# A hybrid retention and DeltaNet layer on one core: query norms from transposes, clears on GpSimd, and a priority for the last attention head

## The chip, the cores and the metric

The kernel runs on one core of a Trainium2 chip. The metric is the device time of one execution in microseconds (us); the time of a kernel is the median of its runs.

Five engines work side by side, each through its own instructions in order: TensorE (PE in the profile: matrix products and transposes into PSUM), VectorE (DVE), ScalarE (ACT), GpSimd (POOL) and SyncE (SP), which here only issues transfers (DMA). Semaphores make one engine wait for another.

## The reference

One encoder layer, batch 1, 256 tokens, width 2048, all in 32-bit floats:

```python
h = rms_norm(x, norm_mix_g)
x = x + hybrid_mixer(h, ...)           # retention and gated DeltaNet
h = rms_norm(x, norm_x_g)
x = x + cross_attention(h, rms_norm(mem, norm_mem_g), w_q, w_kv, w_o)   # 4 heads of 512
h = rms_norm(x, norm_ffn_g)
x = x + jnp.square(jax.nn.relu(h @ w_ff1)) @ w_ff2                      # hidden 8192
out = rms_norm(x, norm_final_g)
```

The change touches the gated DeltaNet and the cross-attention. In the DeltaNet each of 16 heads of width 128 normalises its queries and keys, and then runs the delta rule in chunks of 64 tokens:

```python
gqkv = silu(causal_conv(gqkv, conv_w))
gq, gk, gv = jnp.split(gqkv, ...)
gq = gq * lax.rsqrt(jnp.sum(gq * gq, axis=-1, keepdims=True) + 1e-6) * 128 ** -0.5
gk = gk * lax.rsqrt(jnp.sum(gk * gk, axis=-1, keepdims=True) + 1e-6)
yg = gated_delta_chunked(gq, gk, gv, log_a, beta)   # a triangular solve in each chunk
```

So a sum of squares over the 128 features of a head is needed for each of 256 tokens, of the queries and of the keys. The cross-attention is softmax(q k^T / sqrt(512)) v over 256 memory tokens, head by head, followed by the product with w_o.

## The kernel before

**Weights.** Every dense weight (w_in, w_out, w_xq, w_xkv, w_xo, w_ff1, w_ff2) comes from memory in pieces of 1 MB by the function `fetch`: SP issues the transfer into `raw` (three buffers), ACT rounds each half of it to a high part `whi` (L117, 128x1024), and DVE makes the low part `wlo = raw - whi` (L118). Each of both has three buffers. TensorE multiplies high by high, high by low and low by high, so that products keep nearly the precision of 32 bits. In `blocks`, which makes 256 output features as two PSUM banks s0 and s1, one L200 (a weight's high part by high and low activations side by side, 512 columns) and one L201 (the weight's low part by the high activations, 256 columns) are done for each of 16 input blocks and each of the two banks. The halves of 1024 columns feed eight such pairs. `chunk` does the same with L158 to L160 where the tokens stand on the partitions.

**What sets the order.** The program is written stage by stage, and a scheduler lays out each engine's instructions beforehand by priority and by its own estimate of the time. An instruction's priority is its place in the program, and `tc.high_priority(offset=n)` moves it n places ahead: 100000 in `fetch`, so weights are split as early as their buffers allow, and 50000 for the evacuations of the PSUM banks. Everything else fills what is left. Small results go through `bank()`, one of four PSUM banks under the tag b; s0 and s1 have two each.

**The DeltaNet's stream.** `gdn_stream` handles a group of four heads as two pairs, and runs four times. For each pair it projects queries, keys and values of two heads by `blocks`, convolves them (`conv_silu`, with a 128x256 buffer under the tag acc), and holds keys and queries in `kq`, features on the partitions, and the values in `vt`. Then, for each head: `kh` and `kl`, the high and low parts of keys and queries; `sq`, the square of the queries by ACT (L679, under the tag acc as well); two products of `sq` with a column of `ones` (L686), which sum over the partitions into a few columns of a bank, `ssq`; the products of keys with keys and queries (L688, L690); and the keys' sums of squares from the diagonals (L694). After both heads, `qe4` is made of `ssq` by DVE, `nk` (the keys' lengths) by GpSimd (L704), and, for each head again, ACT copies pieces to `cmp_l` and to the sparse tiles `pair32` and `pair64` (L718 to L725), TensorE transposes `vt` into a bank (L729), and ACT scales it by `nk` into `r4` (L732). `qe4` is read in `gdn_core`, which runs while the next groups' projections stream.

**The triangular solve.** `gdn_blocks` writes `cmp_l` to memory (`scr_l`), reads it back in another layout (`lw`), sets `tw` to the unit matrix (L744, L745) and solves by 31 pairs of DVE instructions (L750, L752). `tw` is one buffer, cleared in each of the four groups. The sparse tiles `pair32`, `pair64`, `t64`, `u64` and `u128` are cleared once (L629), when the pool `mix` opens on memory that the stage before held; `ko` of that stage is still being written to `kt_d` then.

**The cross-attention.** For each of 4 heads: queries, scores, softmax, transposes of the weights `pt`, and then, for two halves d2 of the head's 512 features, twelve value products into one bank (by `three`, L129 to L131; high and low parts of values `vv` and of `pt`), a copy by ACT into the high part of the head's activations `q` (L1080), and a subtraction by DVE for the low part (L1081). Four heads' activations are the input of `blocks` on w_xo, in `residual_pass`; after the last head nothing else is left for TensorE but that product, which reads the first half's activations for its thirteenth and fourteenth blocks of input. `split` is the helper for such a copy and subtraction, and `square_sum` the one for a square with an accumulated sum by ACT.

Of the kernel before, what the change touches and what calls it, by code (L numbers as in the profile page):

```python
# [10 lines left out]
F32 = mybir.dt.float32  # L11
F32R = mybir.dt.float32r
I32 = mybir.dt.int32
AF = mybir.ActivationFunctionType
ALU = mybir.AluOpType
AX = mybir.AxisListType

P = 128
D = 2048
S = 256  # L20
NT = S // P
# [3 lines left out]
GH, GD = 16, 128  # L25
XH, XD = 4, 512
EPS = 1e-6
# [25 lines left out]
def trunk(ctx: ExitStack, tc: tile.TileContext, x_f, mem_f, positions, lead_f, small_f, w_in, ret_gn_g, w_out, w_xq,  # L53
# [3 lines left out]
    act, vec, pool, pe = nc.scalar, nc.vector, nc.gpsimd, nc.tensor  # L57
# [65 lines left out]
    def split(dst, src, at=slice(None)):  # L123
        h, l = (a[:, at] for a in dst)
        act.activation(h, src, AF.Copy)
        vec.tensor_sub(l, src, h.bitcast(F32))

    def three(o, lhs, rhs, first, last):
        pe.matmul(o, lhs[0], rhs[0], start=first, stop=False)  # L129
        pe.matmul(o, lhs[0], rhs[1], start=False, stop=False)  # L130
        pe.matmul(o, lhs[1], rhs[0], start=False, stop=last)  # L131
# [102 lines left out]
    ident = cp.tile([P, P], F32, name="ident")  # L234
    ones = cp.tile([P, P], F32, name="ones")
# [31 lines left out]
    def square_sum(acc, src):  # L267
        junk = sm.tile([P, 512], F32, name="junk", tag="junk", bufs=1)
        act.activation(junk[:, :src.shape[1]], src, AF.Square, accum_out=acc)
# [354 lines left out]
    mx = mixer.enter_context(tc.tile_pool(name="mix", bufs=2))  # L624


    def sparse(nm, *shape):
        t = mx.tile([P, 4, *shape], F32, name=nm, bufs=1)
        vec.memset(t, 0.0)  # L629
        return t  # L630

    pair32, pair64 = sparse("pair32", P), sparse("pair64", P)
# [15 lines left out]
    def gdn_stream(grp):  # L648

        heads = []  # L650
        qe4 = mx.tile([P, 4, NT], F32, name="qe4", tag="qe4", bufs=2)
        for pr in range(2):
            h0 = grp * 4 + pr * 2
            dec = mx.tile([P, 2, 384], F32, name="dec", tag="dec", bufs=1)
            nc.sync.dma_start(dec, dec_d[h0:h0 + 2].rearrange("h p n -> p h n"))
            kq = mx.tile([P, 2, 2, S], F32, name="kq", tag="kq", bufs=1)
            vts = []
            for part, c0, bofs in ((1, C_GQ, 0), (0, C_GK, 16), (2, C_GV, 32)):
                def evac(b, ps, part=part, bofs=bofs):
                    if part < 2:  # L660
                        conv_silu(bofs + h0 + b, ps, kq[:, b, part, :])
                    else:
                        vt = mx.tile([P, S], F32, name="vt", tag="vt", bufs=2)
                        conv_silu(bofs + h0 + b, ps, vt)
                        vts.append(vt)
                blocks(h1, w_in[0], c0 + h0 * GD, 2, evac)
            if pr == 0:
                finish_steps()
                cmp_l = mx.tile([P, 8, 32], F32, name="cmp_l", tag="cmp", bufs=1)
                r4 = mx.tile([P, 4, NT, GD], F32, name="r4", tag="r4", bufs=1)  # L670
            grams = []
            ssk = mx.tile([P, 2, NT], F32, name="ssk", tag="ssk", bufs=2)
            for b in range(2):
                kh = mx.tile([P, 2, S], F32R, name="kh", tag="kh", bufs=2)
                kl = mx.tile([P, 2, S], F32R, name="kl", tag="kl", bufs=2)
                sq = mx.tile([P, S], F32, name="sq", tag="acc", bufs=2)
                act.activation(kh, kq[:, b], AF.Copy)
                vec.tensor_sub(kl, kq[:, b], kh.bitcast(F32))
                act.activation(sq, kq[:, b, 1], AF.Square)  # L679
                g0, g1 = bank(), bank()  # L680
                g0v = g0.rearrange("p (a n) -> p a n", a=2)
                g1v = g1[:, 0:256].rearrange("p (a n) -> p a n", a=2)
                if b == 0:
                    ssq = g1[:, 256:260].rearrange("p (b i) -> p b i", b=2)
                for t in range(NT):
                    pe.matmul(ssq[:, b, t:t + 1], sq[:, t * P:(t + 1) * P], ones[:, :1], start=True, stop=True)  # L686
                for n, (l, r) in enumerate(((kh, kh), (kh, kl), (kl, kh))):
                    pe.matmul(g0v, l[:, 0, 0:P], r, start=n == 0, stop=n == 2)  # L688
                for n, (l, r) in enumerate(((kh, kh), (kh, kl), (kl, kh))):
                    pe.matmul(g1v, l[:, 0, P:S], r[:, :, P:S], start=n == 0, stop=n == 2)  # L690
                grams.append((g0v, g1v))
                for t, src in enumerate((g0v[:, 0, 0:P], g1v[:, 0, :])):
                    dj = sm.tile([P, S], F32, name="dj", tag="bo", bufs=2)[:, :P]
                    vec.scalar_tensor_tensor(dj, src, 1.0, ident, op0=ALU.mult, op1=ALU.mult,  # L694
                                             accum_out=ssk[:, b, t:t + 1])
            ske = mx.tile([P, 2, NT], F32, name="ske", tag="ske", bufs=2)
            vec.tensor_scalar(ske, ssk, EPS, None, op0=ALU.add)
            vec.tensor_scalar(qe4[:, 2 * pr:2 * pr + 2, :], ssq, EPS * GD, EPS * EPS * GD,
                              op0=ALU.mult, op1=ALU.add)
            sc = mx.tile([P, 2, NT], F32, name="sc", tag="sc", bufs=2)  # L700
            vec.reciprocal(sc, ske)
            vec.tensor_mul(sc, sc, beta[:, :, h0:h0 + 2].rearrange("p t h -> p h t"))
            nk = mx.tile([P, 2, NT], F32, name="nk", tag="nk", bufs=2)
            pool.tensor_tensor(nk.rearrange("p b t -> p (b t)"), ske.rearrange("p b t -> p (b t)"), half_pow[:, :4], op=ALU.pow)  # L704
            for b in range(2):
                h, slot = h0 + b, pr * 2 + b
                g0v, g1v = grams[b]

                alt = mx.tile([P, 2, 384], F32, name="alt", tag="alt", bufs=4)
                vec.scalar_tensor_tensor(alt[:, :, 0:S], g0v, sc[:, b, 0:1],  # L710
                                         dec[:, b, 0:256].unsqueeze(1).to_broadcast([P, 2, 256]),
                                         op0=ALU.mult, op1=ALU.mult)
                vec.scalar_tensor_tensor(alt[:, :, S:384], g1v, sc[:, b, 1:2],
                                         dec[:, b, 256:384].unsqueeze(1).to_broadcast([P, 2, P]),
                                         op0=ALU.mult, op1=ALU.mult)
                for q in range(4):
                    ps_ = slice(32 * q, 32 * q + 32)
                    act.activation(cmp_l[ps_, 2 * slot:2 * slot + 2, :], diag(alt)[ps_, :, 32 * q:32 * q + 32], AF.Copy)  # L718

                for t in range(NT):  # L720
                    for a in range(2):
                        to, at = 64 * t + 32 * a, 64 * a
                        act.activation(pair32[to:to + 32, slot, to:to + 32],
                                       diag(alt)[at:at + 32, t, at + 32:at + 64], AF.Copy)
                    act.activation(pair64[64 * t:64 * t + 64, slot, 64 * t:64 * t + 64], diag(alt)[0:64, t, 64:P], AF.Copy)  # L725

                vps = bank()
                for t in range(NT):
                    pe.transpose(vps[:, t * P:(t + 1) * P], vts[b][:, t * P:(t + 1) * P], ident)  # L729
                r = r4[:, slot, :, :]  # L730
                for t in range(NT):
                    act.activation(r[:, t, :], vps[:, t * P:(t + 1) * P], AF.Copy, scale=nk[:, b, t:t + 1])  # L732
                heads.append(alt)
        return heads, cmp_l, r4, qe4

    def gdn_blocks(heads, cmp_l):
# [4 lines left out]
        for q in range(4):  # L741
            nc.sync.dma_start(lw[8 * q:8 * q + 8], scr_l[32 * q:32 * q + 32, :].rearrange("m (g n) -> g m n", g=8))
        tw = mx.tile([32, 32, 32], F32, name="tw", tag="tw", bufs=1)
        vec.memset(tw, 0.0)  # L744
        vec.memset(tw.rearrange("p i c -> p (i c)")[:, ::33], 1.0)  # L745
        for j in range(31):
            n = 31 - j
            pr = mx.tile([32, 272], F32, name="pr", tag="pr", bufs=2)
# [287 lines left out]
    for h in range(XH):  # L1036
# [34 lines left out]
        quad = quad_a()  # L1071
        for d2 in range(2):
            ops = bank()
            ov = ops.rearrange("p (d s) -> p d s", d=2)
            for d in range(2):
                c0 = (2 * d2 + d) * P
                for m in range(NT):
                    three(ov[:, d, :], [a[:, m, c0:c0 + P] for a in vv], [a[:, m, :] for a in pt], m == 0, m == 1)
            qh, ql = (a[:, 2 * d2:2 * d2 + 2, :] for a in quad)
            act.activation(qh, ov, AF.Copy)  # L1080
            vec.tensor_sub(ql, ov, qh.bitcast(F32))  # L1081
        att.append(quad)

    h3, rstd3 = residual_pass(att, w_xo[0], G_FFN, "n3")
# [130 lines left out]
```

## Time and profile before

| what | before |
|---|---|
| median of 3 runs | 2069.61 us (2069.28 to 2069.83) |
| the profiled execution | 2069.25 us |
| its span, first to last instruction | 2067.5 us |
| mean granted TensorE clock | 0.999 |
| memory traffic | 194 GB/s over the span |

The stages by the trace, with the time that TensorE was busy in each:

| stretch, us | stage | TensorE busy, us |
|---|---|---|
| 0 to 110 | memory's norm, first values | 108.54 of 110 |
| 110 to 200 | values and keys of the memory | 90.00 of 90 |
| 200 to 1060 | mixer: retention, DeltaNet, gates | 858.97 of 860 |
| 1060 to 1370 | w_out, cross-attention, w_xo | 309.74 of 310 |
| 1370 to 2067 | MLP, last norm | 689.45 of 697 |

A row of the trace reads: start and duration in us, engine, line, operation, out<-in, the tile's shape, how many; and in brackets how long the engine stood idle before it and what it then waited for. In a view of groups the last column is the idle time before the group. The profile splits one 32-bit product of L686 into two passes. Where matmuls follow closely, each is shown with its whole duration, though the next begins before it ends.

### The profile page before, as it was taken

Reading aid. Unit: us, or ns where it says so; the run is one execution under the profiler, and the core shown is the slowest. Engines: PE = TensorE matmul, PEld = TensorE weight load, DVE = VectorE, ACT = ScalarE, POOL = GpSimd, SP = SyncE. Lnnn points to the kernel's source line nnn. Section 1 sums busy time; section 2 is a strip of 40 time slices with the busy share of each in tenths; the row PEclk is TensorE's granted clock in tenths of the full one; section 3 lists DMA queues with packets and bytes.
Section 4 is the critical chain, followed back from the end, with each engine's and each line's share of the span. In section 5 each row is a group of like instructions: output and inputs, shape, how many; then the busy total and the mean of one; then the engine's idle time right before and its main releaser. Section 6 shows DMA issues by size and latency. Waiting matters only on the chain.

```text
span 2067.5 us, 28359 instructions
## 1 busy us (share of the span) xinstructions
PE 2056.7 (99%) x10954; PEld 1773.0 (86%) x10954; DVE 1420.2 (69%) x2262; ACT 1096.9 (53%) x1739; POOL 30.7 (1%) x37
## 2 busy tenths in 40 slices
PE   9999999999999999999999999999999999999998
PEld 7888888988888888888888898888888888888887
DVE  5887778779667875878567666776556556655654
ACT  5665764675456555755455555554344434434444
POOL 0000000000000000000000000000000000000000
PEclk9999999999999999999999999999999999999999
DMA  9688656555555655565577654689566566566654
GB/s 325 204 261 279 191 179 214 154 187 190 178 171 184 196 178 168 186 188 171 166 223 239 188 184 142 201 202 232 201 187 194 189 194 193 187 200 186 198 187 142
DMA packets 329222, 405.22 MB, mean 196 GB/s; under 512 B 34928, under 2 KB 239360, under 8 KB 328960
## 3 DMA queue, kind: packets, MB, share of 16 engines
q1 hardware_dynamic: 328656, 402.74, 62.5%
q8 instruction: 85, 1.39, 0.3%
q10 hardware_dynamic: 432, 0.69, 0.1%
q14 instruction: 49, 0.40, 0.1%
HBM read 389.74 MB, written 11.55 MB: 194 GB/s over the span
## 4 chain that ended last, share of the span: by engine, by line
PE 99%; DVE 0%; issue 0%; ACT 0%; DMA 0%; POOLq 0%; POOL 0%; ACTq 0%
PE s L200 34%; PE s L201 18%; PE s L159 13%; PE s L158 13%; PE s L160 13%; PE s L384 1%; PE s L386 1%; PE s L385 1%; PE b L781 1%; PE b L688 1%; PE b L814 1%; PE b L130 0%; PE b L129 0%; PE b L131 0%; PE b L690 0%; PE b L686 0%
## 5 line engine op out<-in xcount | busy, mean ns | idle before, releaser
L118 DVE TENSOR_TENSOR wlo<-raw,whi 128x1024 fp32r<-128x1024 f32 x696 | 850.7, 1223 | 495.5 <-ACT whi L117 488.4
L117 ACT ACTIVATE whi<-raw 128x1024 fp32r<-128x1024 f32 x696 | 737.0, 1060 | 698.4 <-PE s L160 347.3
L200 PE MATMUL s<-q,whi 128*128 128x512 f32 x3072 | 1056.7, 391 | 0.3 <-DVE q L1081 0.3
L201 PE MATMUL s<-q,wlo 128*128 128x256 f32 x3072 | 837.5, 281 | 1.0 <-DVE wlo L118 1.0
L200 PEld LDWEIGHTS s<-q,whi 128*128 128x128 f32 x3072 | 566.9, 188 | 109.5 <-DVE q L1081 0.5
L201 PEld LDWEIGHTS s<-q,wlo 128*128 128x128 f32 x3072 | 576.4, 188 | 14.9 <-DVE wlo L118 1.7
L159 PE MATMUL s<-wlo,q 128*128 128x512 f32 (+1 forms) x1200 | 470.4, 392 | 0.0
L160 PE MATMUL s<-whi,q 128*128 128x512 f32 (+1 forms) x1200 | 467.4, 390 | 0.0
L158 PE MATMUL s<-whi,q 128*128 128x512 f32 (+1 forms) x1200 | 427.5, 390 | 0.0
L158 PEld LDWEIGHTS s<-whi,q 128*128 128x128 f32 x1200 | 225.0, 188 | 47.2
L160 PEld LDWEIGHTS s<-whi,q 128*128 128x128 f32 x1200 | 225.4, 188 | 45.7
L159 PEld LDWEIGHTS s<-wlo,q 128*128 128x128 f32 x1200 | 225.5, 188 | 45.3
L207 ACT ACTIVATE bo<-s 128x256 f32<-128x256 f32 x192 | 72.9, 379 | 123.2 <-PE s L201 110.1
L208 DVE TENSOR_TENSOR bo<-bo,s 128x256 f32<-128x256 f32 x192 | 79.9, 416 | 42.0 <-ACT bo L207 41.7
L641 DVE SCALAR_TENSOR_TENSOR acc<-bo,small,acc 128x255 f32<-128x255 f32 (+1 forms) x144 | 66.8, 480 | 3.1 <-ACT acc L638 1.2
L750 DVE TENSOR_TENSOR pr<-lw,tw 32x31 f32<-32x31 f32 (+15 forms) x124 | 40.4, 326 | 8.3 <-DMA lw<-scr_l 6.2
L752 DVE TENSOR_TENSOR tw<-tw,pr 32x31 f32<-32x31 f32 (+15 forms) x124 | 40.5, 327 | 2.0
L1128 DVE SCALAR_TENSOR_TENSOR res<-s,rstd3q,res 128x512 f32<-128x512 f32 (+1 forms) x32 | 22.3, 736 | 12.0 <-PE s L160 12.0
L915 ACT ACTIVATE gth<-s 128x512 f32<-128x512 f32 x32 | 19.0, 593 | 18.1 <-PE s L160 15.1
L1115 DVE SCALAR_TENSOR_TENSOR hs<-bo 128x256 f32<-128x256 f32 x64 | 27.0, 423 | 1.1
L1118 DVE TENSOR_TENSOR q<-hs,q 128x256 fp32r<-128x256 f32 x64 | 26.7, 418 | 0.0
L1117 ACT ACTIVATE q<-hs 128x256 fp32r<-128x256 f32 x64 | 26.1, 409 | 0.6 <-DVE hs L1115 0.6
(310 smaller groups left out, 1178.1 us busy)
## 6 DMA issues: line engine op xcount, KB each, us to landing
raw<-w_in SPq DMA_DIRECT2D x143, 1024.0 KB
raw<-w_ff SPq DMA_DIRECT2D x128, 1024.0 KB
raw<-w_xkv SPq DMA_DIRECT2D x29, 1024.0 KB
raw<-w_out SPq DMA_DIRECT2D x16, 1024.0 KB
raw<-w_xq SPq DMA_DIRECT2D x16, 1024.0 KB
raw<-w_xo SPq DMA_DIRECT2D x16, 1024.0 KB
dec_d<-dec_w SPq DMA_DIRECT2D x8, 384.0 KB
dec<-dec_d SPq DMA_DIRECT2D x8, 384.0 KB
```

The lines of the kernel that those rows point to most:

```text
L117: latest["hi"] = act.activation(hi[:, cs], src[:, cs], AF.Copy).ins
L118: latest["lo"] = vec.tensor_sub(lo[:, cs], src[:, cs], hi[:, cs].bitcast(F32)).ins
L158: pe.matmul(o, xh, wh, start=first, stop=False)
L159: pe.matmul(o, xh, wl, start=False, stop=False)
L160: pe.matmul(o, xl, wh, start=False, stop=last)
L200: pe.matmul(ps[b], lh, xhl, start=kk == 0, stop=False)
L201: pe.matmul(ps[b][:, :S], ll, xh, start=False, stop=kk == KT - 1)
L207: act.activation(o, ps[b][:, S:], AF.Copy)
L208: vec.tensor_add(o, o, ps[b][:, :S])
L641: vec.scalar_tensor_tensor(acc[:, d:], ps[:, :S - d], cw[:, j, blk:blk + 1], acc[:, d:], op0=ALU.mult, op1=ALU.add)
L750: vec.tensor_mul(pv, lw[:, j, j + 1:32].unsqueeze(2).to_broadcast([32, n, j + 1]), tw[:, j, 0:j + 1].unsqueeze(1).to_broadcast([32, n, j + ...
L752: vec.tensor_sub(tw[:, j + 1:32, 0:j + 1], tw[:, j + 1:32, 0:j + 1], pv)
```

## The change

Three things are done.

1. The queries are no longer squared with features on the partitions. TensorE transposes them as well, into the free half of the bank that takes the transposed values (new L723; the values' transposes are now L721), and ACT squares and sums each 128x128 half in one instruction with an accumulator (`square_sum`, new L269) into a small tile `ssq`. The tile `sq`, its square and the products with `ones` are gone. `qe4` is made at the end of the pair.
2. The clears of the sparse tiles (L629) and of `tw` (new L742, L743) are issued to GpSimd, not to DVE.
3. The value products of the last attention head, and the copy and subtraction that follow, get a priority 20000 places ahead. The other heads keep theirs, and `split` now stands for the two written-out instructions.

```diff
@@ sparse
         t = mx.tile([P, 4, *shape], F32, name=nm, bufs=1)
-        vec.memset(t, 0.0)
+        pool.memset(t, 0.0)
@@ gdn_stream
-            ssk = mx.tile([P, 2, NT], F32, name="ssk", tag="ssk", bufs=2)
+            ssk, ssq = (mx.tile([P, 2, NT], F32, name=nm, tag=nm, bufs=2) for nm in ("ssk", "ssq"))
             for b in range(2):
...
-                sq = mx.tile([P, S], F32, name="sq", tag="acc", bufs=2)
                 act.activation(kh, kq[:, b], AF.Copy)
                 vec.tensor_sub(kl, kq[:, b], kh.bitcast(F32))
-                act.activation(sq, kq[:, b, 1], AF.Square)
...
-                if b == 0:
-                    ssq = g1[:, 256:260].rearrange("p (b i) -> p b i", b=2)
-                for t in range(NT):
-                    pe.matmul(ssq[:, b, t:t + 1], sq[:, t * P:(t + 1) * P], ones[:, :1], start=True, stop=True)
...
-            vec.tensor_scalar(qe4[:, 2 * pr:2 * pr + 2, :], ssq, EPS * GD, EPS * EPS * GD,
-                              op0=ALU.mult, op1=ALU.add)
...
                 for t in range(NT):
                     pe.transpose(vps[:, t * P:(t + 1) * P], vts[b][:, t * P:(t + 1) * P], ident)
+                for t in range(NT):
+                    pe.transpose(vps[:, S + t * P:S + (t + 1) * P], kq[:, b, 1, t * P:(t + 1) * P], ident)
                 r = r4[:, slot, :, :]
                 for t in range(NT):
                     act.activation(r[:, t, :], vps[:, t * P:(t + 1) * P], AF.Copy, scale=nk[:, b, t:t + 1])
+                for t in range(NT):
+                    square_sum(ssq[:, b, t:t + 1], vps[:, S + t * P:S + (t + 1) * P])
                 heads.append(alt)
+            vec.tensor_scalar(qe4[:, 2 * pr:2 * pr + 2, :], ssq, EPS * GD, EPS * EPS * GD,
+                              op0=ALU.mult, op1=ALU.add)
@@ gdn_blocks
-        vec.memset(tw, 0.0)
-        vec.memset(tw.rearrange("p i c -> p (i c)")[:, ::33], 1.0)
+        pool.memset(tw, 0.0)
+        pool.memset(tw.rearrange("p i c -> p (i c)")[:, ::33], 1.0)
@@ the heads of the cross-attention
-            for d in range(2):
-                c0 = (2 * d2 + d) * P
-                for m in range(NT):
-                    three(ov[:, d, :], [a[:, m, c0:c0 + P] for a in vv], [a[:, m, :] for a in pt], m == 0, m == 1)
-            qh, ql = (a[:, 2 * d2:2 * d2 + 2, :] for a in quad)
-            act.activation(qh, ov, AF.Copy)
-            vec.tensor_sub(ql, ov, qh.bitcast(F32))
+            with tc.high_priority(offset=20000 if h == XH - 1 else 0):
+                for d in range(2):
+                    c0 = (2 * d2 + d) * P
+                    for m in range(NT):
+                        three(ov[:, d, :], [a[:, m, c0:c0 + P] for a in vv], [a[:, m, :] for a in pt], m == 0, m == 1)
+                split([a[:, 2 * d2:2 * d2 + 2, :] for a in quad], ov)
```

What the change does to the order of the instructions shows at three places. The first is TensorE at the end of the first pair of the first group (a row is a line, an operation and out<-in with the shape of the output, and how many of the same stand there). Before, the products with ones and the transposes stand apart between the projections of the next pair:

```order
L200 MATMUL s_2375<-q,whi 128x512
L686 MATMUL b<-ones,sq 128x1 x2
L201 MATMUL s_2375<-q,wlo 128x256
L200 MATMUL s_2376<-q,whi 128x512
L201 MATMUL s_2376<-q,wlo 128x256
```

```order
L200 MATMUL s_2376<-q,whi 128x512
L729 MATMUL b<-ident,vt 128x128 x2
L201 MATMUL s_2376<-q,wlo 128x256
L200 MATMUL s_2375<-q,whi 128x512
L201 MATMUL s_2375<-q,wlo 128x256
L729 MATMUL b<-ident,vt 128x128 x2
L200 MATMUL s_2376<-q,whi 128x512
```

Now the values' and the queries' transposes of both heads stand in one run:

```order
L200 MATMUL s_2277<-q,whi 128x512
L201 MATMUL s_2277<-q,wlo 128x256
L721 MATMUL b<-ident,vt 128x128 x2
L723 MATMUL b<-ident,kq 128x128 x2
L721 MATMUL b<-ident,vt 128x128 x2
L723 MATMUL b<-ident,kq 128x128 x2
L200 MATMUL s_2276<-q,whi 128x512
```

The rows with `sq` are gone, and the run of eight stands a little ahead of where the values' transposes stood.

The second place is DVE where the pool `mix` opens, after the last block of the memory's keys. This is one piece of the difference, - for before and + for now:

```order
 L612 TENSOR_TENSOR ko<-bo,nm_row 128x256
-L118 TENSOR_TENSOR wlo<-raw,whi 128x1024
-L629 MEMSET pair_1853 128x512
-L629 MEMSET pair_1855 128x512
-L629 MEMSET t_1857 128x256
-L629 MEMSET u_1859 128x256
-L629 MEMSET u_1861 128x1024
-L744 MEMSET tw 32x1024
-L118 TENSOR_TENSOR wlo<-raw,whi 128x1024 x2
-L745 MEMSET tw 32x32
+L118 TENSOR_TENSOR wlo<-raw,whi 128x1024 x3
 L208 TENSOR_TENSOR bo<-bo,s_1867 128x256
```

The low parts of three halves of a weight now follow each other with nothing between them.

The third place is TensorE at the end of the last attention head, ahead of the product with w_xo. The tile names tell the two halves' banks apart. Before (b_12085 is the first half's bank, b_12100 the second's):

```order
L129 MATMUL b_12085<-pth_11842,vvh_11838 128x256
L130 MATMUL b_12085<-ptl_11843,vvh_11838 128x256
L131 MATMUL b_12085<-pth_11842,vvl_11839 128x256
L130 MATMUL b_12100<-ptl_11843,vvh_11838 128x256
L131 MATMUL b_12100<-pth_11842,vvl_11839 128x256
L129 MATMUL b_12100<-pth_11842,vvh_11838 128x256
```

and now (b_12125 is the first half's bank, b_12140 the second's):

```order
L129 MATMUL b_12125<-pth_11882,vvh_11878 128x256
L129 MATMUL b_12140<-pth_11882,vvh_11878 128x256
L130 MATMUL b_12125<-ptl_11883,vvh_11878 128x256
L130 MATMUL b_12140<-ptl_11883,vvh_11878 128x256
L131 MATMUL b_12125<-pth_11882,vvl_11879 128x256
L131 MATMUL b_12140<-pth_11882,vvl_11879 128x256
L200 MATMUL s0_12158<-q_12124,whi_12208 128x512
```

Before, the first half's products were done before all but one of the second half's; now the products of the two halves alternate to the end, and the first half's last product is the last but one ahead of L200.

## The prediction

> **What bounds the kernel now.** The first view is the page's busy line, then its chain of waits:
>
> ```profile
> PE 2056.7 (99%) x10954; PEld 1773.0 (86%) x10954; DVE 1420.2 (69%) x2262; ACT 1096.9 (53%) x1739; POOL 30.7 (1%) x37
> PE 99%; DVE 0%; issue 0%; ACT 0%; DMA 0%; POOLq 0%; POOL 0%; ACTq 0%
> ```
>
> TensorE is busy for 2056.7 of 2067.5 us and the chain that ends last is TensorE for 99% of it. So a change can win time in two ways only: fewer or cheaper passes on TensorE, or fewer places where TensorE waits. The view of waits, for TensorE, tells how little there is of the second kind inside the stages that change:
>
> ```profile
> PE s L201 <- DVE wlo L118: 1.0, 1, 1.0
> PE s L200 <- DVE q L1081: 0.3, 1, 0.3
> ```
>
> One wait of 1.0 us for a low half of a weight, one of 0.3 us for the low half of an attention output. Both turn out to be touched by the change. Work moved between the other engines is worth nothing unless it ends or makes such a wait.
>
> **Part 1, removed: the sums of queries by ones.** The group of all such products, and one place of the TensorE timeline (start, duration, instruction):
>
> ```profile
> L686 PE MATMUL b<-ones,sq 128*128 128x1 f32 x64 | 8.0, 229 | 0.0
> 241.91 0.40 PE L200 MATMUL s<-q,whi 128*128 128x512 f32 x1
> 242.14 0.51 PE L686 MATMUL b<-ones,sq 128*128 128x1 f32 x4
> 242.51 0.36 PE L201 MATMUL s<-q,wlo 128*128 128x256 f32 x1
> 242.71 0.39 PE L200 MATMUL s<-q,whi 128*128 128x512 f32 x1
> 242.94 0.28 PE L201 MATMUL s<-q,wlo 128*128 128x256 f32 x1
> 243.05 0.40 PE L200 MATMUL s<-q,whi 128*128 128x512 f32 x1
> ```
>
> Matmuls overlap, so a duration is not a price; the distance from start to start is. One L200 with one L201 takes 243.05 - 242.71 = 0.34 us. With four passes of L686 between them it takes 242.71 - 241.91 = 0.80. Four passes cost 0.46, and the 64 in the trace (two passes for each of the 32 products) 16 x 0.46 = 7.4 us. All of it lies on TensorE, which is the bound.
>
> **Part 1, added: the queries' transposes.** There are 2 for each of 16 heads, 32 in all. The nearest row is the transpose of the values, of the same shape and already in the kernel; a run of six transposes from another stage shows its pace:
>
> ```profile
> L729 PE MATMUL b<-ident,vt 128*128 128x128 f32 x32 | 6.1, 272 | 0.0
> 492.93 0.28 PE L201 MATMUL s<-q,wlo 128*128 128x256 f32 x1
> 493.05 0.82 PE L261 MATMUL b<-ident,yg 128*128 128x128 f32 x6
> 493.62 0.48 PE L200 MATMUL s<-q,whi 128*128 128x512 f32 x1
> 493.93 0.28 PE L201 MATMUL s<-q,wlo 128*128 128x256 f32 x1
> ```
>
> From L201 to L201 pass 1.00 us; 0.34 of it are the ordinary pair, so six transposes cost 0.66, one 0.11. They are one pass each, where a product by ones was two. 32 x 0.11 = 3.5 us; the upper bound is the busy time of the 32 transposes of values, 6.1 us. I take 3.5, as start to start is the price on a full queue, and the new transposes stand in a run of eight behind those of the values, whose operands have long been there. Part 1 on TensorE: 3.5 - 7.4 = **-3.9 us**, bounds -4.1 and 6.1 - 7.4 = -1.3.
>
> The Trainium skill, "TensorE: Matmul & The Clock Gate", Part 4: PE-mode transpose, speaks against this part: it gives about 275 ns for a transpose in one kernel's context. The 272 ns of L729 agree with it as a duration; by it as a price the 32 would cost an estimated 8.8 us, part 1 would lose 1.4 and the sum would be 2070.7. The run of six says that transposes overlap, so I don't follow it.
>
> **Part 1, on ACT and DVE.** Per head ACT loses one square of 128x256 and gets two of 128x128 with a read of the accumulator, for which the kernel has a twin at L833:
>
> ```profile
> L679 ACT ACTIVATE sq<-kq 128x256 f32<-128x256 f32 x16 | 6.7, 420 | 0.5
> L833 ACT ACTIVATE junk<-b 128x128 f32<-128x128 f32 x32 | 8.9, 278 | 12.2 <-PE b L827 7.6 <-PE b L830 3.8
> L833 ACT ACTIVATION_READ_ACCUMULATOR junk<-b 128x1 f32 x32 | 6.2, 195 | 0.0
> L732 ACT ACTIVATE r<-b,nk 128x128 f32<-128x128 f32 x32 | 9.6, 367 | 0.1
> 254.71 1.06 ACT L117 ACTIVATE whi<-raw 128x1024 fp32r<-128x1024 f32 x1 [0.68 <-PE s L200]
> ```
>
> That is 2 x (0.28 + 0.19) - 0.42 = 0.52 us more per head, 8.3 over the kernel, on an engine that is busy 53%. What hides it is the ring of three buffers for high halves: at 254.71, after the first pair's copies, ACT again waits 0.68 us for TensorE to give one back, so it is ahead. I cost it at nothing; the price without that cover is the last rival. DVE does the same tensor_scalar for qe4, later; its readers come a whole group later. The products of keys (L688, L690) no longer share a buffer tag with the squares and start some products earlier; they are the same products, so nothing is won by that on a full TensorE.
>
> **Part 2, the clears on GpSimd.** The view of time around the one wait for a low half (TensorE, DVE, ACT):
>
> ```profile
> 202.81 0.63 PE L200 MATMUL s<-q,whi 128*128 128x512 f32 x2
> 204.46 0.51 PE L201 MATMUL s<-q,wlo 128*128 128x256 f32 x2 [1.03 <-DVE wlo L118]
> 204.81 0.40 PE L200 MATMUL s<-q,whi 128*128 128x512 f32 x1
> 197.37 1.06 ACT L117 ACTIVATE whi<-raw 128x1024 fp32r<-128x1024 f32 x1 [1.65 <-PE s L200]
> 199.62 1.02 DVE L629 MEMSET pair<- 128x512 f32 x2 [2.65 <-DMA kt_d<-ko]
> 202.42 0.91 DVE L744 MEMSET tw<- 32x1024 f32 x1
> 203.26 1.15 DVE L118 TENSOR_TENSOR wlo<-raw,whi 128x1024 fp32r<-128x1024 f32 x1
> ```
>
> The high half was ready at 198.43. DVE stood at the first clear until 199.62, because that memory is still read by a transfer to kt_d, then cleared until 203.26, and only then made the low half for which TensorE stopped. Without the stop the L201 would have begun at 202.81 + 2 x 0.23 = 203.27 instead of 204.46: 1.19; it then needs 0.11 more than its 0.24 to come back to pace. With the wait and the clears on GpSimd DVE can begin the subtraction at 198.5 and has 4.7 us to spare: **-1.3 us**. Bounds: 0 if the clear on GpSimd holds DVE, and -1.3. On GpSimd nothing stands behind these clears but nk of the first pair, 40 us later (240.51). The clears of tw in the other groups cost TensorE nothing now and save nothing.
>
> **Part 3, the last head's value products.** Timelines of TensorE, ACT and DVE at the end of the last attention head:
>
> ```profile
> 1282.69 0.28 PE L131 MATMUL b<-pth,vvl 128*128 128x256 f32 x1
> 1282.81 0.28 PE L130 MATMUL b<-ptl,vvh 128*128 128x256 f32 x1
> 1284.01 0.28 PE L131 MATMUL b<-pth,vvl 128*128 128x256 f32 x1
> 1284.56 0.50 PE L200 MATMUL s<-q,whi 128*128 128x512 f32 x1 [0.27 <-DVE q L1081]
> 1283.01 0.60 ACT L1080 ACTIVATE q<-b 128x512 fp32r<-128x512 f32 x1 [0.37 <-PE b L131]
> 1282.68 1.23 DVE L118 TENSOR_TENSOR wlo<-raw,whi 128x1024 fp32r<-128x1024 f32 x1 [1.78 <-ACT whi L117]
> 1283.82 0.68 DVE L1081 TENSOR_TENSOR q<-b,q 128x512 fp32r<-128x512 f32 x1
> ```
>
> The first bank's last product starts at 1282.69; its copy, subtraction and release take until the L200 at 1284.56, 1.87 us. Meanwhile TensorE runs the second bank's last eleven products, 0.12 us each ((1284.01 - 1282.81) / 10), and could have gone on at 1284.13: it loses 0.43. The order of the changed kernel shows what the priority does: the two banks' products now alternate, so the first bank's last product is followed by a single one of the second. Ten products of cover, 1.2 us, are gone. The subtraction need not stand behind a weight's any more (the copy ended at 1283.61, the subtraction began at 1283.82), so the 1.87 become about 1.7, and 1.7 - 0.24 = 1.45 are lost instead of 0.43: **+1.0 us**. Bounds: +1.2 with no quicker subtraction; -0.4 if the scheduler's order did not bind and the wait went away. The second bank's split follows 0.7 us behind the first's, and four pairs of 0.34 lie before TensorE needs it, so it costs nothing.
>
> **Part 4, a wait that stays.** The triangular solve's first product waits on DVE for a transfer, with weights' subtractions behind it:
>
> ```profile
> 297.72 0.18 DVE L750 TENSOR_TENSOR pr<-lw,tw 32x31 f32<-32x31 f32 x1 [2.19 <-DMA lw<-scr_l]
> ```
>
> It happens in four groups, and TensorE does not stop at any. DVE no longer clears tw (0.91 us), so it comes to this wait earlier, but leaves it when the transfer lands, as before. I take 0; at worst 0.5 us of each of the four show, +2.0.
>
> **The sum.** -3.9 - 1.3 + 1.0 = -4.2 us. The profiled execution took 2069.25 (its span of 2067.5 and 1.75 around it), 0.36 under the median of the runs shown; from the execution 2065.05 follow, from the median 2069.61 - 4.2 = **2065.4 us**.
>
> **Rivals.**
> (a) The clears still hold DVE back. For it: GpSimd and DVE do disturb each other in this trace, as the same small power takes 0.70 us in one place and 1.99 in another:
>
> ```profile
> 320.89 1.99 POOL L250 TENSOR_TENSOR rg<-ve,nhalf_pow 128x2 f32<-128x2 f32 x1 [42.95 <-DVE ve L902]
> 537.37 0.70 POOL L250 TENSOR_TENSOR rg<-ve,nhalf_pow 128x2 f32<-128x2 f32 x1 [87.92 <-DVE ve L902]
> ```
>
> Against it: there it is GpSimd that is slowed, and 4.7 us are spare. Price: the 1.3 are not won, 2066.7. The Trainium skill, "SBUF — State Buffer", section "Who interferes with whom", says that a DVE instruction with two SBUF inputs contends with a GpSimd instruction that reads SBUF, not with one that only writes; a clear only writes, so by it this rival falls, and no row here shows a clear beside a subtraction.
> (b) The priority does what its name says: TensorE no longer waits at the last head. 0.43 won instead of 1.0 lost, 2064.0. Against it stands the alternation, which an engine that runs in order must follow.
> (c) The solve's wait shows on TensorE: 2067.4 by part 4.
> (d) Transposes cost their busy time or more: 6.1 instead of 3.5, 2068.0; with the 272 ns of L729 each, 8.7 instead of 3.5, 2070.6.
> (e) Slower: ACT's backlog. In each of the eight pairs of heads ACT must do four scaled copies (0.30 each of busy time, 9.6 / 32) and now four squares of 0.47, 1.9 us more in the stretch in which it is most loaded, while high halves queue behind. It decides where a pair's delay exceeds the 0.68 us by which ACT was ahead at 254.71: 1.9 - 0.7 = 1.2 us a pair, 9.6 in all, 2075.0. Against it: in the new order two of a pair's squares stand behind the first high half after the copies, not ahead of it, and the other square of each head is gone from before; and TensorE has two further buffers to eat, 8 pairs of 0.34 each.
>
> **How the numbers follow.** The forecast has 0.58, (a) 0.06, (b) 0.14, (c) 0.08, (d) 0.04, (e) 0.10. 0.2% of the time, about what a measurement of this kernel can tell from no change, is 4.1 us: faster means below 2065.5. The forecast lies on that bound; I give 0.33 of its 0.58 to faster. With (b): 0.47 faster. Within: 0.25 + 0.06 + 0.08 + 0.04 = 0.43. Slower: (e), 0.10. The range leaves (e) and (d) out above and reaches from under (b) to over (c): 2063.4 to 2068.0.
>
> **What would show it.** L686 is gone, 64 transposes stand where 32 stood, and start to start eight of them cost 0.9 us; TensorE's busy time falls by 3 to 4 us. No wait of TensorE for a low half near 203; the first clear on GpSimd begins near 199.6. At the last head a wait of L200 for the split of about 1.3 to 1.5 us instead of 0.3. ACT's high halves still wait for TensorE after each pair. The prediction is wrong if new waits for high or low halves appear in the stage from 230 to 900 us, or if the wait at the last head does not grow.

## The result, and the profile after

| what | before | after |
|---|---|---|
| median of 22 runs each, us | 2069.77 (2068.67 to 2072.33) | 2066.70 (2064.82 to 2068.26) |
| ratio, 95% interval | | 0.9985 [0.9979, 0.9991] |
| profiled execution, us | 2069.25 | 2066.57 |
| its span, us | 2067.5 | 2064.8 |

The kernel became faster by 3.1 us (0.15%), 1.9 to 4.3 by the interval; 4.2 were forecast, and of the chances in the prediction it is the 0.43 for a change of under 0.2% that came true, not the 0.47 for more. The page's busy line and the view of TensorE's waits of the changed kernel:

```profile
PE 2054.2 (99%) x10922; PEld 1769.7 (86%) x10922; DVE 1412.2 (68%) x2249; ACT 1096.4 (53%) x1787; POOL 37.4 (2%) x50
PE s L200 <- DVE q L126: 1.3, 1, 1.3
PE s L384 <- DVE q L319: 0.5, 1, 0.5
```

The wait for a low half near 204 us is gone, and the wait at the last head has grown from 0.3 to 1.3 us. Both were in the sum. The last line is a wait in the first 135 us, of 0.4 us before. TensorE's busy time fell by 2.5 us, not by 3 to 4, and ACT's did not grow by 8.3 us but stayed as it was (1096.9 before). The timelines of the four places follow, first TensorE at the first pair's transposes (start, duration, instruction):

```profile
236.94 0.28 PE L201 MATMUL s<-q,wlo 128*128 128x256 f32 x1
237.06 0.38 PE L721 MATMUL b<-ident,vt 128*128 128x128 f32 x2
237.28 0.38 PE L723 MATMUL b<-ident,kq 128*128 128x128 f32 x2
237.50 0.38 PE L721 MATMUL b<-ident,vt 128*128 128x128 f32 x2
237.71 0.38 PE L723 MATMUL b<-ident,kq 128*128 128x128 f32 x2
237.85 0.48 PE L200 MATMUL s<-q,whi 128*128 128x512 f32 x1
238.16 0.28 PE L201 MATMUL s<-q,wlo 128*128 128x256 f32 x1
238.28 0.39 PE L200 MATMUL s<-q,whi 128*128 128x512 f32 x1
```

From 237.06 to 238.28 pass 1.22 us; less the ordinary pair of 0.34, eight transposes cost 0.88, 0.11 each, as the run of six had it before. The about 275 ns that the Trainium skill ("TensorE: Matmul & The Clock Gate", Part 4: PE-mode transpose) gives fit a single transpose's duration here (272 ns for L721) and are no price in a run.

GpSimd and DVE at the clears:

```profile
199.10 0.99 POOL L629 MEMSET pair<- 128x512 f32 x2 [103.86 <-DMA kt_d<-ko]
200.29 1.21 POOL L629 MEMSET u<- 128x256 f32 x2
198.09 1.22 DVE L118 TENSOR_TENSOR wlo<-raw,whi 128x1024 fp32r<-128x1024 f32 x1 [1.48 <-ACT whi L117]
200.85 1.23 DVE L118 TENSOR_TENSOR wlo<-raw,whi 128x1024 fp32r<-128x1024 f32 x1 [1.54 <-ACT whi L117]
```

The wait for the transfer now stands on GpSimd, and DVE makes its low halves meanwhile. The subtraction at 200.85 runs beside a clear and takes 1.23 us, the mean of all of them being 1.22: rival (a) falls, as the rule of the Trainium skill had it ("SBUF — State Buffer", section "Who interferes with whom": two SBUF inputs on DVE contend with a GpSimd instruction that reads, not with one that only writes).

TensorE and ACT at the last head:

```profile
1280.36 0.40 PE L130 MATMUL b<-ptl,vvh 128*128 128x256 f32 x2
1280.60 0.40 PE L131 MATMUL b<-pth,vvl 128*128 128x256 f32 x2
1282.30 0.50 PE L200 MATMUL s<-q,whi 128*128 128x512 f32 x1 [1.30 <-DVE q L126]
1280.92 1.08 ACT L125 ACTIVATE q<-b 128x512 fp32r<-128x512 f32 x2 [1.57 <-PE b L131]
```

From the first half's last product at 1280.60 to L200 it takes 1.70 us, where 1.7 was reckoned. Two products of 0.12, itself and the one behind it, fill 0.24 us of that, and 1.46 are lost.

The fourth place was not in the sum. This is the group of L200 in the stage of w_out, from 1080 to 1157 us in both traces, with the number of products (the number behind the shape counts every second one) and the shortest, the median and the longest duration in ns; first the kernel before, then the changed one:

```profile
L200 PE MATMUL s<-q,whi x224: 387/389/396, 1079.9 to 1156.8; 128*128 128x512 f32 x112
```

```profile
L200 PE MATMUL s<-q,whi x220: 391/398/398, 1079.8 to 1157.0; 128*128 128x512 f32 x110
```

In the same 77 us TensorE gets through 220 instead of 224 of these products, the median 9 ns longer, in a stage that the change does not touch, with no wait in it and the granted clock at 1.00. Start to start, L200 to L201 takes 226.7 ns before and 235.7 after, L201 to L200 117 to 118 in both.

Where the time went is seen when both traces are laid over each other by the same product of a weight (each kernel has the same 10038 of them, in nearly the same order). The change in the start of the same product over a stretch, in us, with all the runs of the next section; times of the bounds are those of the kernel before, and the column "from 1161" ends with the last of these products, about 8 us ahead of the span's end:

| kernel | to 135 | 135 to 212 | 212 to 1076 | 1076 to 1161 (w_out) | from 1161 | sum from 135 | ratio to before, 95% interval |
|---|---|---|---|---|---|---|---|
| changed kernel | -0.38 | -1.33 | -3.48 | +1.92 | +1.00 | -1.89 | 0.9985 [0.9979, 0.9991] |
| e1 queries alone | -0.11 | -0.43 | -3.63 | +1.93 | +0.03 | -2.10 | 0.9990 [0.9981, 0.9998] |
| e2 clears alone | -0.20 | -1.33 | -0.05 | +0.01 | -0.01 | -1.38 | 0.9991 [0.9982, 0.9999] |
| e3 priority alone | -0.46 | -0.21 | 0.00 | +0.39 | +1.10 | +1.28 | 1.0002 [0.9993, 1.0011] |
| e4 without priority | +0.72 | -1.33 | -3.29 | +1.93 | +0.03 | -2.66 | 0.9983 [0.9974, 0.9992] |
| e5 changed, one product more | +1.19 | -1.33 | -3.48 | +0.12 | +1.04 | -3.65 | 0.9982 [0.9973, 0.9990] |
| e6 before, four passes more | -0.54 | -0.29 | +0.44 | +0.01 | +0.07 | +0.23 | 1.0001 [0.9992, 1.0009] |
| e7 changed, halves in order | +1.21 | -1.33 | -3.71 | +1.92 | +0.04 | -3.08 | 0.9983 [0.9974, 0.9991] |
| e8 e4, one product more | -0.16 | -1.33 | -3.57 | +0.12 | +0.01 | -4.77 | 0.9974 [0.9964, 0.9983] |
| e9 before again | +0.48 | -0.15 | 0.00 | 0.00 | +0.07 | -0.08 | 0.9998 [0.9989, 1.0007] |
| e10 changed again | -0.26 | -1.33 | -3.62 | +1.93 | +1.01 | -2.01 | 0.9987 [0.9978, 0.9996] |
| e11 e8, two products more | +1.40 | -1.33 | -3.34 | +0.12 | -0.24 | -4.79 | 0.9975 [0.9965, 0.9985] |

Behind 135 us the stages repeat to a few hundredths from execution to execution (e9 against before, e10 against the changed kernel), but for the old wait at 204 us, which moves with its transfer, and some tenths among the groups of the DeltaNet. The first 135 us differ by up to 1.9 us between executions of the same order of products there. The intervals of the ratios are over 1 us wide on each side, so the traces tell more than the medians here.

The table leaves out the end of the span. From the last of the products to the last instruction it takes 8.33 to 8.37 us in the five traces with the clears on DVE (before, e1, e3, e6, e9) and 7.92 to 7.95 in the eight with the clears on GpSimd. So part 2 wins a further 0.4 us there that nobody forecast. The difference lies between GpSimd's two semaphore instructions in the closing exchange of all engines, 0.44 us apart before and 0.08 in the changed kernel; what shortens it was not settled.

### The profile page after: what moved, and what is told of

Its sections match the earlier page's. It is cut to its first block, busy times and chain, and to the rows that moved or that the text cites. A ratio compares the mean times of both kernels' runs of the same rounds, so it can differ in the third digit from the quotient of the medians.

```text
span 2064.8 us, 28349 instructions
## 1 busy us (share of the span) xinstructions
PE 2054.2 (99%) x10922; PEld 1769.7 (86%) x10922; DVE 1412.2 (68%) x2249; ACT 1096.4 (53%) x1787; POOL 37.4 (2%) x50
## 4 chain that ended last, share of the span: by engine, by line
PE 98%; DMA 1%; DVE 0%; issue 0%; ACT 0%; SPq 0%; POOLq 0%; POOL 0%; ACTq 0%; DVEq 0%
PE s L200 34%; PE s L201 18%; PE s L159 13%; PE s L160 13%; PE s L158 13%; DMA raw<-w_xkv 1%; PE b L779 1%; PE b L682 1%; PE b L130 1%; PE b L812 1%; PE b L129 1%; PE b L131 1%; PE s L385 0%; PE b L684 0%; PE s L386 0%; PE s L384 0%
## 5 line engine op out<-in xcount | busy, mean ns | idle before, releaser
L118 DVE TENSOR_TENSOR wlo<-raw,whi 128x1024 fp32r<-128x1024 f32 x696 | 850.7, 1223 | 493.3 <-ACT whi L117 484.0
L200 PE MATMUL s<-q,whi 128*128 128x512 f32 x3072 | 1059.1, 391 | 1.3 <-DVE q L126 1.3
L201 PE MATMUL s<-q,wlo 128*128 128x256 f32 x3072 | 836.8, 281 | 0.0
L200 PEld LDWEIGHTS s<-q,whi 128*128 128x128 f32 x3072 | 566.8, 188 | 112.4 <-DVE q L126 1.5
L201 PEld LDWEIGHTS s<-q,wlo 128*128 128x128 f32 x3072 | 576.9, 188 | 13.9 <-DVE wlo L118 0.4
L207 ACT ACTIVATE bo<-s 128x256 f32<-128x256 f32 x192 | 73.2, 381 | 112.9 <-PE s L201 112.8
L638 ACT ACTIVATE acc<-bo,small 128x256 f32<-128x256 f32 x48 | 24.7, 514 | 7.7 <-DVE bo L208 7.6
```

The source lines that it names most:

```text
L118: latest["lo"] = vec.tensor_sub(lo[:, cs], src[:, cs], hi[:, cs].bitcast(F32)).ins
L200: pe.matmul(ps[b], lh, xhl, start=kk == 0, stop=False)
L201: pe.matmul(ps[b][:, :S], ll, xh, start=False, stop=kk == KT - 1)
L207: act.activation(o, ps[b][:, S:], AF.Copy)
```

## The experiments

**e1, the queries alone.** Parts 2 and 3 undone:

```diff
-        pool.memset(t, 0.0)
+        vec.memset(t, 0.0)
...
-            with tc.high_priority(offset=20000 if h == XH - 1 else 0):
+            qh, ql = (a[:, 2 * d2:2 * d2 + 2, :] for a in quad)
+            act.activation(qh, ov, AF.Copy)
+            vec.tensor_sub(ql, ov, qh.bitcast(F32))
```

> Part 1 of the change alone; TensorE's order up to the last head is the changed kernel's. Theory 'pace': the new order ahead of the product with w_out leaves TensorE in a slower pace for that whole stage (start to start of L200 to L201 235.7 ns in the changed kernel's trace, 226.7 before), which gives back 2.0 us of the 3.6 that the queries save: 1.6 us under before, and L200 to L201 near 235.7 ns in the w_out stage. Rival 'chance': the pace falls at random in each execution, so this profile may show 226.7 ns there and the time is 2.6 to 3.6 us under before. Rival 'no pace': the transposes simply cost more than counted; then the eight in a run take over 1.3 us and not 0.9.

Measured: a median of 2067.68, 1.9 us under before, and the median L200 in the w_out stage 398 ns:

```profile
L200 PE MATMUL s<-q,whi x220: 391/398/399, 1079.7 to 1157.0; 128*128 128x512 f32 x110
```

So the slower pace comes with part 1, not with the clears or the priority. The time alone could not have told it from the rival 'chance': the interval reaches from 0.4 to 3.9 us.

**e2, the clears alone.** The three lines with `pool.memset` in the kernel before.

> Part 2 alone. My sum: TensorE's wait of 1.0 us near 204 us is gone and the time falls by 1.3 us, w_out at the old pace (226.7 ns). Rival 'GpSimd holds DVE': the wait stays or the subtraction is slowed, the time is that of before within 0.3 us.

Measured: -1.33 us where the wait was, nothing elsewhere in the table, and the 0.4 us at the end of the span; the median is 2067.43, 2.1 under before, and the ratio's interval reaches from 0.2 to 3.7 us. My term stands.

**e3, the priority alone.** The `with` block of part 3 in the kernel before.

> Part 3 alone. My sum: a wait of L200 of 1.3 us at the last head instead of 0.3, the time 1.0 us over before, w_out at the old pace (226.7 ns). Rival 'priority helps': the wait goes away, 0.4 us under before.

The largest line of the view of TensorE's waits of this kernel behind 135 us:

```profile
PE s L200 <- DVE q L126: 1.3, 1, 1.3
```

+1.10 us at the last head; the median of 2070.40 alone (0.9 us over) could not tell this from nothing. The +0.39 in w_out is a single stop at 1084 us: a weight load waits 0.55 us for a low half by DVE (L118), whose high half stood on ACT behind a wait for a transfer (`vr`, 2.10 us here and 1.06 before).

**e4, parts 1 and 2 without the priority.**

```diff
-            with tc.high_priority(offset=20000 if h == XH - 1 else 0):
...
-                split([a[:, 2 * d2:2 * d2 + 2, :] for a in quad], ov)
+            qh, ql = (a[:, 2 * d2:2 * d2 + 2, :] for a in quad)
+            act.activation(qh, ov, AF.Copy)
+            vec.tensor_sub(ql, ov, qh.bitcast(F32))
```

> Parts 1 and 2 without part 3. My sum with the pace: the changed kernel without the 1.0 us lost at the last head, 4.1 us under before (3.1 measured for the whole change, and 1.0), with the wait at the last head back at 0.3 us and w_out still at 235.7 ns. Rival 'chance' for the pace: 226.7 ns there, and up to 6.1 us under before.

The last head costs 0.03 instead of 1.00, and w_out stays slow (+1.93). The median of 2066.76 is 2.8 us under before, where 4.1 were expected; the ratio's interval, 1.7 to 5.4 us, holds both. Its profile has +0.72 in the first 135 us; the trace's sum behind them, -2.66, is 0.8 below the changed kernel's.

**e5, one product more in the changed kernel.** Behind the first two output blocks of w_out:

```diff
+                if extra and kk == KT - 1:
+                    pe.matmul(bank()[:, :S], lh, xh, start=True, stop=True)
...
-            blocks(quads, w, b2 * 256, 2, evac)
+            blocks(quads, w, b2 * 256, 2, evac, extra=name == "n2" and b2 == 0)
```

> The changed kernel with one product of 128x256 added into a bank that nobody reads, behind the first two output blocks of the product with w_out; nothing else in TensorE's order moves there. Theory 'the products inserted between the pairs set the pace': a product of 256 columns brings TensorE back to 226.7 ns from L200 to L201, for some 215 pairs of 9 ns: 1.9 us less, 0.1 us for the product: 1.8 us under the changed kernel, 4.9 under before. Rival 'something else of the stage (addresses, transfers) slows it': 235.7 ns stays, 0.1 us over the changed kernel.

TensorE's timeline around the added product (L203):

```profile
1072.15 0.40 PE L200 MATMUL s<-q,whi 128*128 128x512 f32 x1
1072.38 0.28 PE L201 MATMUL s<-q,wlo 128*128 128x256 f32 x1
1072.50 0.40 PE L200 MATMUL s<-q,whi 128*128 128x512 f32 x1
1072.74 0.28 PE L201 MATMUL s<-q,wlo 128*128 128x256 f32 x1
1072.85 0.28 PE L203 MATMUL b<-q,whi 128*128 128x256 f32 x1
1072.97 0.39 PE L200 MATMUL s<-q,whi 128*128 128x512 f32 x1
1073.20 0.28 PE L201 MATMUL s<-q,wlo 128*128 128x256 f32 x1
1073.31 0.39 PE L200 MATMUL s<-q,whi 128*128 128x512 f32 x1
```

Ahead of it L200 to L200 takes 0.35 us and L200 lasts 0.40; behind it 0.34 and 0.39, and so it stays to the end of the stage. +1.92 became +0.12, which is what the product itself costs: 1.8 us won, as expected. The median is 2066.07, 4.1 us under before where 4.9 were expected, within the interval of 2.1 to 5.6. The weights, the activations and, but for two neighbouring products, the order of TensorE's other products in the stage are the same, so none of these by itself holds the stage in the slow pace. Addresses are not in the traces.

**e6, four small passes more in the kernel before,** at the same place:

```diff
+                if extra and kk == KT - 1:
+                    e = bank()
+                    for c in range(2):
+                        pe.matmul(e[:, c:c + 1], ident, ones[:, :1], start=True, stop=True)
```

> The kernel before with two small 32-bit products (four passes, as of L686) added at the same place. Theory 'inserted products set the pace': L200 to L201 goes from 226.7 to 235.7 ns until the next products at the end of the stage, some 215 to 250 pairs of 9 ns, 1.9 to 2.2 us, and 0.5 us for the four passes: 2.4 to 2.7 us over before. Rival 'something else of the stage': 226.7 ns stays, 0.5 us over before.

A miss: +0.44 for the passes, no slower pace, and a median of 2070.06 against 2070.14. Four such passes are no sure switch into it; at this place two L200 in a row follow them, where L200 and L201 by turns follow the products by ones behind which the slower pace came.

**e7, the last head's halves in order.**

```diff
-            with tc.high_priority(offset=20000 if h == XH - 1 else 0):
+            with tc.high_priority(offset=20000 - 10000 * d2 if h == XH - 1 else 0):
```

> The changed kernel with 20000 places for the last head's first half and 10000 for its second, so that the two halves' products no longer alternate. Theory 'the alternation costs, not the priority': the wait of L200 at the last head falls from 1.3 us to 0.1 to 0.3, the time by 1.0 to 1.2 us under the changed kernel; w_out stays at 235.7 ns. Rival 'the split itself is late': the wait stays above 1 us.

The wait of this kernel at the last head:

```profile
PE s L200 <- DVE q L126: 0.3, 1, 0.3
```

+0.04 instead of +1.00 there: the alternation costs, not the priority. The medians (2066.34 and 2066.70) do not show it; this profile has 1.21 us more in the first 135 us.

**e8, e4 with the added product of e5.**

> Parts 1 and 2 without the priority, and with the added product of 128x256 behind the first output blocks of w_out. If both losses are what I take them for: 1.0 and 1.8 us under the changed kernel, 5.5 to 6 us under before, w_out at 226.7 ns, a wait of 0.3 us at the last head. If the pace is not set there: 2.8 to 4 us under before.

2064.14 us, 6.0 under the median of the kernel before that ran with it, and 5.4 by the ratio of 0.9974 [0.9964, 0.9983]; 5.5 to 6 were expected. The trace gives -4.77 behind 135 us, 2.9 below the changed kernel, and w_out has the fast pace.

**e9 and e10, both kernels once more.**

> The kernel before, unchanged, timed as if it were a changed one and profiled again. Theory 'the first 110 us vary from execution to execution, all else repeats': from 135 us on every stage takes what it took in the first profile within 0.1 us (last head, w_out at 226.7 ns), except for the wait at 204 us, which moves with the transfer ahead of it by some tenths; the ratio is 1.000 within 0.0005. Rival 'the comparison favours whatever is submitted': 0.6 us under before, as the sums of the trace's stages lie above the medians by about that in the runs so far.

> The changed kernel, unchanged, profiled and timed again. Theory 'the pace follows from the order': w_out at 235.7 ns in this execution too, the last head's wait 1.3 us, and the stages from 135 us on as in its first profile within 0.1 us, 1.9 us under before; rival 'chance': 226.7 ns. The time is 2 to 3 us under before.

e9 is at 0.9998: two sets of runs of one kernel show no difference, though with 1.9 us on each side the 0.6 us of the rival could not be excluded. In the kernels with part 2, 0.4 of those 0.6 us are the end of the span, which the sums of the stages leave out. e10 has w_out at +1.93 again. In the five traces with part 1 and no added product (the changed kernel twice, e1, e4, e7) the stage was slow, in all others fast: the pace goes with the program and not with chance.

**e11, two more products** behind the sums of squares that end the residual passes:

```diff
+        one = nxt[0].both[:, 0, :]
+        pe.matmul(bank()[:, :S], one[:, :P], one[:, :S], start=True, stop=True)
```

> Parts 1 and 2 without the priority, with the added product behind the first output blocks of w_out and one more product of 128x256 behind each of the two sums of squares by ones that end the residual passes, where the trace shows the slower pace for 36 and 27 pairs. If a product of 256 columns sets the faster pace everywhere: 0.2 and 0.1 us less than without the two, 226.7 ns in both places; if only in w_out: 0.2 us more.

From 1161 us on it takes 0.24 us less than before, e8 0.01 more: the quarter of a microsecond is there in the trace. The median, 2064.71, cannot tell it from e8. Both are faster than the kernel before; that they are faster than the changed one rests on the traces and on medians 2.0 to 2.6 us lower, as the intervals of the ratios touch.

## Why the prediction was right, and which term it lacked

- **The bound.** TensorE set the end nearly throughout; ACT's added squares cost nothing anywhere (rival (e) fell: no wait for a high half in the mixer, and ACT's busy time did not grow), and the solve's wait never reached TensorE (rival (c) fell). Transposes in a run cost 0.11 us, and the first clears slowed no subtraction, so (d) and (a) fell too.
- **Part 1 on TensorE,** -3.9: the six other traces with part 1 and the two of the changed kernel give -3.3 to -3.7 in the mixer. The run of eight costs what was reckoned. The missing 0.2 to 0.6 was not isolated. The products of keys now stand one by one between pairs, and pairs next to them take up to 10 ns longer; that this is the rest is only argued.
- **Part 2,** -1.3: measured -1.33, alone and together, against the first trace of the kernel before. The wait moves with its transfer: in the four other traces with the clears on DVE the same stretch is 0.15 to 0.44 shorter, so this part is worth 0.9 to 1.3 us there. The 0.4 at the end of the span come on top and were not in the sum.
- **Part 3,** +1.0: measured +1.00, +1.01, and +1.10 alone. Rival (b), to which I gave 0.14, had no ground once the order was read. The products of the other heads alternate too in the changed kernel, at no cost (e7: +0.04), since there other products of weights follow.
- **The step that failed** is the use of 0.34 us for an ordinary pair wherever it stands, and with it that a stage without a changed instruction costs nothing. A pair has more than one price. In w_out the pairs went at 353 instead of 345 ns: +1.92 over a stretch of 247 pairs, which the sum did not have. The rows that hint at it were on the page: in the first fence of part 1, L200 lasts 0.39 us at 242.71 and 0.40 at 243.05, behind the products by ones, and the slower pace then held until the next inserted products.
- **What starts the slower pace stays open.** TensorE's order does not differ there: from 1024 to 1197 us of the kernel before both kernels have the same products and transposes one for one. Up to 1069 us their distances agree to 2 ns. At two transposes near 1069.5 us they part by 3 to 5 ns, in the same way both times for each kernel, and behind the next place where two L200 follow each other, near 1074 us, the one goes on at 224 to 231 ns from L200 to L201 and the other at 235 to 236. It comes with part 1 (e1), but whether by the addresses of its tiles, by the place of the instructions in the program or by the other engines' times, no run here separates.
- **The sum** was -4.2. With the pace and the end of the span, the measured terms make -3.5 - 1.33 + 1.92 + 1.00 - 0.42 = -2.3. The medians say -3.1, and -2.7 the second time, with intervals of 1.2 and 1.9 us on each side that hold it; both profiled spans are 2.7 shorter. The rest, if it is one, lies ahead of 135 us; why that stretch would be shorter in the changed kernel was not settled. That the time lies in the range is in part luck: the bounds were drawn for rivals (b) and (c), neither of which happened, and had room for a loss of 1.9 us that nobody forecast.

## What to carry to other kernels

When an engine that is full sets the end, the price of an instruction there is the distance from start to start, and it has to be read in each stage of the new trace as well, those that the change does not touch included: lay both traces over each other by the same product, up to the span's end, and a gain that was lost or won elsewhere shows at once. A priority given to a block of code can also dissolve the order inside it; where one half is waited for, give the halves different priorities. Differences under 0.1% are told by such an overlay, stage by stage, where the medians do not tell them yet; how well a stage repeats has to be seen from a second trace of the same kernel.

## What the hardware showed

TensorE has more than one steady pace for the same alternation of products of 512 and 256 columns, at a granted clock of 1.00: 345 ns a pair (226.7 and 118) or 353 ns (235.7 and 117.5) for the same order of products in w_out, and 347 ns (230 and 117) behind some of the products of keys in the changed kernel (229 to 237 us). The slow pace lasted 92 us around w_out, across sixteen evacuations of PSUM banks (L207), up to the next small products. Behind the four passes near 1366 us of the kernel before it lasted only 27 pairs, and ended at 1376.4 us, where four L200 follow each other, with no small product in between.

The second distance behind a run of small products tells which pace follows. Where the first L200 to L201 took 313 or 314 ns and the next L201 to L200 113 or 114, it was the slow one, in all 32 such places of the thirteen traces (six transposes at 1066.76 in the changed kernel; four passes at 1163.05 before). Where the latter took 116 ns or more it was not (six transposes at 1071.99 before: 316 and 117). One product of 256 columns brought the fast pace back in each of the places tried, for 0.12 us. What in the engine makes the paces, no run here tells.
